# The DRAM round trip of the triangular solve: fewer, wider transfers with an even pitch, in a streaming encoder step

## The chip, the core and the metric

The kernel runs on one core of a Trainium2 chip. The metric is device time in microseconds of one execution. Engines are named as in the profile: PE (TensorE), DVE (VectorE), ACT (ScalarE), POOL (GpSimd) and SP (SyncE, which issues every DMA of this kernel).

## The reference, cut to what matters

One inference step of a one-layer encoder: 2048 prompt tokens and 32 sample tokens of width 1024. After an RMSNorm and the projection `w_in`, the columns go to window attention and to RWKV-7 time mixing; then come `w_out`, cross-attention to 256 memory tokens, and an MLP of width 4096. The change lies in the RWKV part, a recurrence over tokens for each of 8 heads:

```python
def step(S, inp):
    r_t, w_t, k_t, v_t, a_t, b_t = inp
    sa = jnp.einsum('bhij,bhj->bhi', S, a_t)
    S = S * w_t[:, :, None, :] + sa[..., None] * b_t[:, :, None, :] + v_t[..., None] * k_t[:, :, None, :]
    return S, jnp.einsum('bhij,bhj->bhi', S, r_t)
```

The kernel doesn't step token by token. It takes chunks of 64 tokens; within a chunk the term `sa` makes each token depend on the ones before it, which is a unit-triangular system of 64x64 for each head and chunk. Its inverse is what the code below calls the solve.

## The kernel before

**The whole.** A plan written as a string lists the phases in order: Y and Z (projection by `w_in`), R (an RWKV tile of 128 tokens, two chunks; one more, Rs, holds the 32 sample tokens), A (attention), O, C, X, D (output projection and cross-attention), and the MLP behind them. There are 17 RWKV tiles. Each phase runs under a priority, and a scheduler that plans with a timeline of its own lays all instructions out, engine by engine, in a fixed order; each engine then runs its row in that order. So an instruction that waits holds up all that stands behind it on its engine. The dense phases' matmuls (`ps_z`, 24 to a block, three for each of eight weight slices) are the filler between the RWKV tiles' small ones.

**An RWKV tile.** `rwkv_tile` forms `z` and `bk`, multiplies them into `pA`, and ACT copies the triangular part into `ab`: 128 partitions (two heads' 64 rows) by 8 (head pair and chunk) by 64 columns. Then the solve, at highest priority:

- L648 to L650: the 16x16 blocks on the diagonal, 64 of them, go out to the DRAM scratch `lscr`, one block after the other, in eight stores: partitions 16k to 16k+15, all 8 matrices, 16 columns.
- L651 to L653: one gather brings them back as `lt`, one block to a partition, twice (partitions 0 to 63 and 64 to 127).
- L654 to L663: DVE inverts all blocks at once by 15 steps of elimination, each a product into `prd` and an addition into `xt`. The two halves of the partitions hold the even and the odd rows of the inverse.
- L664 to L666: two stores put `xt` into the scratch `xscr`, again block after block.
- L667 to L671: POOL clears `td`, and eight loads put the inverted blocks back on the diagonal, 16 partitions each.
- From L673: a transpose on DVE (`xn`), the matmuls `pgm` and `ptm`, and the same once more widen the 16x16 inverses to 32 and then to 64 rows in `tm`. The serial part over the chunks (`pW`, `pU`, `pS`, `py`) and the normalisation follow.

The scratch tensors `lscr` and `xscr` are made anew for each tile. At the start of the program, POOL clears the eight buffers `rt` (L510). SP's first loads are `par`, then the first token block `xb`, from which PE's first matmuls come.

Of the kernel before, what the change touches and what calls it, by code (L numbers as in the profile page):

```python
# [10 lines left out]
F32 = mybir.dt.float32  # L11
# [6 lines left out]
P = 128  # L18
# [32 lines left out]
def hymba_step_kernel(  # L51
# [9 lines left out]
    V, G, S, T, Q = nc.vector, nc.gpsimd, nc.scalar, nc.tensor, nc.sync  # L61
# [6 lines left out]
    def tt(out, a, b, op, eng=None):  # L68
        (eng or V).tensor_tensor(out, a, b, op=op)  # L69
# [7 lines left out]
    dram = ctx.enter_context(tc.tile_pool(name="dram", bufs=1, space=DRAM))  # L77
# [128 lines left out]
    def setp(k):  # L206
        prs[pcur[0]] = tc.cur_priority
        old, pcur[0] = pcur[0], k
        tc.cur_priority = prs[k]
        return old  # L210
# [39 lines left out]
    rp = rctx.enter_context(tc.tile_pool(name="rp", bufs=1))  # L250
# [204 lines left out]
    def xajob(rp, g, h, t0, tl, src, nb=1, tq=None, tt_=None):  # L455
        sc_f = 128.0 ** -0.5
        if True:
# [47 lines left out]
    rtz = [[[rp.tile([P, 4, 64], F32, name=f"rt{q}{c}{e}", bufs=1) for e in range(2)] for c in range(2)]  # L505
           for q in range(2)]
    for q in range(2):
        for c in range(2):
            for e in range(2):
                G.memset(rtz[q][c][e], 0.0)  # L510
    rcount = [0]

    def halves():
# [2 lines left out]
    def rwkv_tile(g, lo, valid, key, last):  # L516
# [123 lines left out]

        lab(rl_ + "sol")
        pold = setp(PSOL)
        lscr = dram.tile([64, 16, 16], F32, name=f"lscr_{g}_{lo}")
        xscr = dram.tile([64, 16, 16], F32, name=f"xscr_{g}_{lo}")
        if nch == 1:
            V.memset(ab[:, :, 1, :], 0.0)
        ab8 = ab.rearrange("p a c x -> p (a c) x")
        for k in range(8):  # L648
            r0, x0 = 16 * k, 16 * (k % 4)
            Q.dma_start(lscr[8 * k:8 * k + 8].rearrange("q s t -> s q t"), ab8[r0:r0 + 16, :, x0:x0 + 16])  # L650
        lt = rp.tile([P, 16, 16], F32, tag="lt", name="lt", bufs=1)  # L651
        lsr = lscr[:, :, :]
        Q.dma_start(lt, bass.AP(lsr.tensor, lsr.offset, [[0, 2], [256, 64], [1, 256]]))  # L653
        xt = rp.tile([P, 8, 16], F32, tag="xt", name="xt", bufs=1)  # L654
        V.tensor_copy(xt, xt0.rearrange("p (a b) -> p a b", a=8))
        for s in range(15):
# [4 lines left out]
            tt(pv_, xt[:, 0:ni, s:s + 1].broadcast_to([P, ni, m]),  # L661
               lt[:, s, None, s + 1:16].broadcast_to([P, ni, m]), MUL)
            tt(xt[:, 0:ni, s + 1:16], xt[:, 0:ni, s + 1:16], pv_, ADD)  # L663
        xs2 = xscr.rearrange("n (i q) t -> q n i t", q=2)  # L664
        for q in range(2):
            Q.dma_start(xs2[q], xt[64 * q:64 * q + 64])  # L666
        td = rp.tile([P, 8, 32], F32, tag="td", name="td", bufs=1)  # L667
        G.memset(td, 0.0)
        for k in range(8):
            r0, x0 = 16 * k, 16 * (k % 2)  # L670
            Q.dma_start(td[r0:r0 + 16, :, x0:x0 + 16], xscr[8 * k:8 * k + 8].rearrange("q r t -> r q t"))  # L671
        st = 3 - nch
        blk = [(pr, c) for c in range(nch) for pr in range(4)]  # L673
        tm = rp.tile([P, 4, 2, 64], F32, tag="tm", name="tm", bufs=TMB)
# [190 lines left out]
    def rstep(g, i):  # L865
        if g == "s":
            s0 = rp.tile([P, 4, 64], F32, tag="sn", name="sn_s", bufs=SNB)
            Q.dma_start(s0, swkv)
            st8["s"] = (s0, None, None)
            rwkv_tile(0, 0, NS, "s", swo)  # L870
        else:
            if g == 0 and i == 0:
                p0 = rp.tile([P, 4, 64], F32, tag="sn", name="sn_p", bufs=SNB)
                V.memset(p0, 0.0)
                st8["p"] = (p0, None, None)
            lo = i * P + (NS if g == 0 else 0)
            rwkv_tile(g, lo, P, "p", pwkv if (g == 3 and i == 3) else None)
# [43 lines left out]
    for it in PLAN.split():  # L921
        k = it[0]
# [5 lines left out]
        elif k in "RA":  # L928
            g = it[1] if it[1] == "s" else int(it[1])
# [235 lines left out]
```

## Time and profile before

| | |
|---|---|
| three timed runs | 3285.52, 3291.79, 3298.22 us (median 3291.79) |
| profiled execution | 3291.38 us, of which the span from first to last instruction is 3289.6 |
| PE busy | 3046.8 us, 93% of the span |
| DVE, ACT, POOL busy | 58%, 38%, 31% |
| mean granted TensorE clock | 0.958 |

The page gives busy time by engine, 40 equal slices of the span (82.2 us each), the chain of work that ended last, and the costliest groups. The views behind it cut the span into stretches, list waits by who waited for whom, and show instructions one by one. A busy share of PE counts a matmul that runs at half clock as busy too.

### The profile page before, as it was taken

What the parts mean: (1) busy time and instruction counts of PE and PEld (TensorE: products, weight loads), DVE (VectorE), ACT (ScalarE), POOL (GpSimd) and SP (SyncE); (2) the same over time, 40 slices, a digit from 0 to 9 for tenths busy, and PEclk for the clock granted to TensorE, in tenths of its full rate; (3) what the DMA queues carried; (4) which work ended last, traced back from release to release, by engine and by line L of the source; (5) the groups of instructions that cost most, each with busy time, mean ns of one, the idle gap of its engine ahead of it and who ended that gap; (6) DMA issues with size and microseconds to landing.
All of it is one profiled execution on the core that took longest, in us unless ns stands there. A gap on an engine that the chain in (4) does not pass through costs nothing.

```text
span 3289.6 us, 64991 instructions
## 1 busy us (share of the span) xinstructions
PE 3046.8 (93%) x25605; PEld 2851.5 (87%) x25605; DVE 1895.3 (58%) x4482; ACT 1247.3 (38%) x2824; POOL 1018.4 (31%) x1034
## 2 busy tenths in 40 slices
PE   8988888888978998889988999999999999999998
PEld 7877766777767887778978999999999999999998
DVE  4577887876777566774334644444446654444446
ACT  5354555443454454445443312222224322222223
POOL 3543353334344343434444511111112521111111
PEclk9989988999989999989989999999999999999999
DMA  5433333323333453436766211111113211111112
GB/s 174 137 87 96 95 115 106 89 86 109 103 108 109 130 161 105 118 98 205 229 213 197 75 41 46 46 52 40 52 39 105 72 52 46 45 52 52 44 47 90
DMA packets 338660, 317.98 MB, mean 97 GB/s; under 512 B 84490, under 2 KB 260146, under 8 KB 338354
## 3 DMA queue, kind: packets, MB, share of 16 engines
q1 hardware_dynamic: 338354, 313.83, 31.1%
q8 instruction: 201, 3.29, 0.4%
q14 instruction: 105, 0.86, 0.1%
HBM read 245.21 MB, written 68.77 MB: 95 GB/s over the span
## 4 chain that ended last, share of the span: by engine, by line
PE 63%; DVE 15%; DMA 11%; ACT 4%; issue 3%; SPq 2%; POOL 1%; DVEq 0%; ACTq 0%; POOLq 0%
PE ps_up L236 7%; PE ps_dn L995 7%; PE ps_up L235 7%; PE ps_up L234 7%; PE ps_dn L997 7%; PE ps_dn L996 7%; PE ps_z L234 4%; PE ps_z L236 4%; PE ps_z L235 4%; DMA lt<-lscr 3%; DVE z L69 2%; DVE prd L69 1%; DVE xt L69 1%; DMA xscr<-xt 1%; SPq L650 1%
## 5 line engine op out<-in xcount | busy, mean ns | idle before, releaser
L234 PE MATMUL ps_z<-xh,w_h 128*128 128x256 f32 (+1 forms) x2368 | 721.7, 305 | 81.2 <-DVE zo L69 31.8
L235 PE MATMUL ps_z<-xl,w_h 128*128 128x256 f32 (+1 forms) x2368 | 711.3, 300 | 1.8 <-DVE xl L72 1.8
L236 PE MATMUL ps_z<-xh,w_l 128*128 128x256 f32 (+1 forms) x2368 | 708.2, 299 | 0.0
L66 ACT ACTIVATE w_h<-w_raw 128x512 fp32r<-128x512 f32 x576 | 345.3, 626 | 794.5 <-PE ps_up L235 258.5
L69 DVE TENSOR_TENSOR x<-ps_dn,x 128x352 f32<-128x352 f32 (+1 forms) x768 | 389.6, 516 | 365.8 <-PE ps_dn L997 362.1
L234 PEld LDWEIGHTS ps_z<-xh,w_h 128*128 128x128 f32 x2368 | 474.9, 201 | 106.5 <-DVE zo L69 27.7
L69 POOL TENSOR_TENSOR w_l<-w_raw,w_h 128x512 fp32r<-128x512 f32 x300 | 396.3, 1335 | 550.5 <-ACT w_h L66 513.4
L69 POOL TENSOR_TENSOR rl<-rl 128x352 f32<-128x352 f32 (+1 forms) x192 | 161.5, 842 | 1136.9 <-ACT uh L66 1136.9
L236 PE MATMUL ps_up<-fh,w_l 128*128 128x352 f32 (+1 forms) x1536 | 495.6, 323 | 1.3 <-DVE w_l L69 1.2
L995 PE MATMUL ps_dn<-uh,w_h 128*128 128x352 f32 (+1 forms) x1536 | 492.9, 321 | 4.1 <-DVE x L69 3.0
L996 PE MATMUL ps_dn<-ul,w_h 128*128 128x352 f32 (+1 forms) x1536 | 490.8, 320 | 4.9 <-DVE ul L69 4.9
L234 PE MATMUL ps_up<-fh,w_h 128*128 128x352 f32 (+1 forms) x1536 | 493.3, 321 | 0.4 <-DVE zo L69 0.4
L235 PE MATMUL ps_up<-fl,w_h 128*128 128x352 f32 (+1 forms) x1536 | 491.1, 320 | 0.5 <-DVE fl L72 0.5
L997 PE MATMUL ps_dn<-uh,w_l 128*128 128x352 f32 (+1 forms) x1536 | 490.5, 320 | 0.0
L235 PEld LDWEIGHTS ps_z<-xl,w_h 128*128 128x128 f32 x2368 | 474.1, 200 | 18.5 <-issue 11.0
L236 PEld LDWEIGHTS ps_z<-xh,w_l 128*128 128x128 f32 x2368 | 473.9, 200 | 13.4 <-issue 9.4
L69 DVE TENSOR_TENSOR w_l<-w_raw,w_h 128x512 fp32r<-128x512 f32 x276 | 198.4, 738 | 228.1 <-ACT w_h L66 228.0
L996 PEld LDWEIGHTS ps_dn<-ul,w_h 128*128 128x128 f32 x1536 | 289.6, 189 | 5.5 <-DVE ul L69 5.2
L995 PEld LDWEIGHTS ps_dn<-uh,w_h 128*128 128x128 f32 x1536 | 288.7, 188 | 6.1 <-DVE x L69 2.5
L236 PEld LDWEIGHTS ps_up<-fh,w_l 128*128 128x128 f32 x1536 | 288.4, 188 | 2.1 <-DVE w_l L69 1.9
L235 PEld LDWEIGHTS ps_up<-fl,w_h 128*128 128x128 f32 x1536 | 288.5, 188 | 1.1 <-DVE fl L72 0.8
L234 PEld LDWEIGHTS ps_up<-fh,w_h 128*128 128x128 f32 x1536 | 288.2, 188 | 1.2 <-DVE zo L69 0.6
(246 smaller groups left out, 4516.7 us busy)
## 6 DMA issues: line engine op xcount, KB each, us to landing
w_raw<-in_win SPq DMA_DIRECT2D x160, 256.0 KB, 3.0
w_raw<-in_wup SPq DMA_DIRECT2D x136, 256.0 KB, 2.7
w_raw<-in_wdn SPq DMA_DIRECT2D x136, 256.0 KB, 2.9
w_raw<-in_wout SPq DMA_DIRECT2D x64, 256.0 KB, 3.6
zrw<-zo SPq DMA_DIRECT2D x84, 128.0 KB, 3.4
zin<-zrw SPq DMA_DIRECT2D x16, 512.0 KB
w_raw<-in_wcq SPq DMA_DIRECT2D x32, 256.0 KB, 3.4
w_raw<-in_wco SPq DMA_DIRECT2D x32, 256.0 KB, 3.3
```

Source lines behind the costliest of these rows:

```text
L66: S.activation(out, in_, func, **kw)
L69: (eng or V).tensor_tensor(out, a, b, op=op)
L234: T.matmul(ps, lhsT=a, rhs=c, start=(k == 0), stop=False)
L235: T.matmul(ps, lhsT=a, rhs=d, start=False, stop=False)
L236: T.matmul(ps, lhsT=b, rhs=c, start=False, stop=(k == nk - 1))
L650: Q.dma_start(lscr[8 * k:8 * k + 8].rearrange("q s t -> s q t"), ab8[r0:r0 + 16, :, x0:x0 + 16])
L995: T.matmul(ps[:, 0:n], lhsT=wh[:, ms], rhs=us[i][0], start=(i == 0), stop=False)
L996: T.matmul(ps[:, 0:n], lhsT=wh[:, ms], rhs=us[i][1], start=False, stop=False)
L997: T.matmul(ps[:, 0:n], lhsT=wl[:, ms], rhs=us[i][0], start=False, stop=(i == 1))
```

## The change

The scratch takes a form in which whole rows can be moved.

- **Out.** `lscr` holds whole 64x64 matrices, 4160 numbers apart; block n of 16x16 then begins at 1040 n, and its rows are 64 apart. `ab` goes out whole, in two stores of 64 partitions (each 64 x 8 pieces of 64 numbers). Stored before were the diagonal blocks alone.
- **Gather.** Two loads, one for each half of `lt`, take 976 numbers in a row for each of the 64 blocks: its 16 rows of 64, of which the elimination reads the first 16 columns. `lt` is now 1024 wide instead of 256.
- **Inverse back.** `xscr` has a pitch of 32 to a row and 528 to a block, so that two blocks stand on the diagonal of a 32x32 matrix. Two such scratch tensors are made once, filled with zeros by four stores at the start of the program, and used in turn. The two stores of `xt` write the blocks; the zeros beside them stay. Four loads bring 32 partitions of `td` each, zeros included, and the memset of `td` is gone.

```diff
+    xscrs = [dram.tile([64, 528], F32, name=f"xscr{q}") for q in range(2)]
+    for q in range(2):
+        xz = xscrs[q][:, :]
+        zr_ = rtz[0][0][0].rearrange("p a b -> p (a b)")
+        Q.dma_start(bass.AP(xz.tensor, xz.offset, [[256, P], [1, 256]]), zr_)
+        Q.dma_start(bass.AP(xz.tensor, xz.offset + 256 * P, [[256, 4], [1, 256]]), zr_[0:4])
...
-        lscr = dram.tile([64, 16, 16], F32, name=f"lscr_{g}_{lo}")
-        xscr = dram.tile([64, 16, 16], F32, name=f"xscr_{g}_{lo}")
+        lscr = dram.tile([64, 1040], F32, name=f"lscr_{g}_{lo}")
...
-        for k in range(8):
-            r0, x0 = 16 * k, 16 * (k % 4)
-            Q.dma_start(lscr[8 * k:8 * k + 8].rearrange("q s t -> s q t"), ab8[r0:r0 + 16, :, x0:x0 + 16])
-        lt = rp.tile([P, 16, 16], F32, tag="lt", name="lt", bufs=1)
-        lsr = lscr[:, :, :]
-        Q.dma_start(lt, bass.AP(lsr.tensor, lsr.offset, [[0, 2], [256, 64], [1, 256]]))
+        lsr = lscr[:, :]
+        for h in range(2):
+            Q.dma_start(bass.AP(lsr.tensor, lsr.offset + 4160 * h, [[64, 64], [8320, 8], [1, 64]]),
+                        ab8[64 * h:64 * h + 64])
+        lt_ = rp.tile([P, 1024], F32, tag="lt", name="lt", bufs=1)
+        lt = lt_.rearrange("p (a b) -> p a b", a=16)
+        for q in range(2):
+            Q.dma_start(lt_[64 * q:64 * q + 64, 0:976], lscr[:, 0:976])
...
-        xs2 = xscr.rearrange("n (i q) t -> q n i t", q=2)
+        xscr = xscrs[rcount[0] % 2]
+        xsr = xscr[:, :]
         for q in range(2):
-            Q.dma_start(xs2[q], xt[64 * q:64 * q + 64])
+            Q.dma_start(bass.AP(xsr.tensor, xsr.offset + 32 * q, [[528, 64], [64, 8], [1, 16]]),
+                        xt[64 * q:64 * q + 64])
         td = rp.tile([P, 8, 32], F32, tag="td", name="td", bufs=1)
-        G.memset(td, 0.0)
-        for k in range(8):
-            r0, x0 = 16 * k, 16 * (k % 2)
-            Q.dma_start(td[r0:r0 + 16, :, x0:x0 + 16], xscr[8 * k:8 * k + 8].rearrange("q r t -> r q t"))
+        for k in range(4):
+            Q.dma_start(td[32 * k:32 * k + 32], bass.AP(xsr.tensor, xsr.offset + 1056 * k, [[32, 32], [4224, 8], [1, 32]]))
```

The scheduler lays the whole program out anew, so the order moves on every engine. On SP, in tile R11 (128 tokens from column 128 of group 1; `w_raw` are weight loads, `zrw` stores of projections), the order before was:

```order
L650 DMA lscr_128_8735<-ab 16x8x16 x8
L361 DMA zrw_92<-zo 128x256
L653 DMA lt<-lscr_128_8735 128x1x256
L257 DMA w_raw<-in_win 128x512
L361 DMA zrw_92<-zo 128x256
L257 DMA w_raw<-in_win 128x512
L529 DMA zv<-zrw_91 128x4x128
L361 DMA zrw_92<-zo 128x256
L666 DMA xscr_128_8736<-xt 512x1x16 x2
L527 DMA zl<-zrw_91 128x2x128
L671 DMA td<-xscr_128_8736 16x8x16 x8
```

The same place on SP in the changed kernel:

```order
L655 DMA lscr_128_8675<-ab 64x8x64 x2
L660 DMA lt<-lscr_128_8675 64x976 x2
L361 DMA zrw_92<-zo 128x256
L257 DMA w_raw<-in_win 128x512
L535 DMA zv<-zrw_91 128x4x128
L361 DMA zrw_92<-zo 128x256
L257 DMA w_raw<-in_win 128x512
L870 DMA mscr_95<-ao 128x4x128
L800 DMA vf<-zqkv_87 128x128
L674 DMA xscr_144<-xt 64x8x16 x2
L533 DMA zl<-zrw_91 128x2x128
L678 DMA td<-xscr_144 32x8x32 x4
```

The gather stands directly behind the stores, where a `zrw` store stood between; other loads moved to between the gather and the xscr stores.

On DVE in the same tile, from the last product out of `pA` (`z`) to the first elimination step (`prd`), before:

```order
L69 TENSOR_TENSOR z_8641<-pA,cst 64x512
L846 TENSOR_SCALAR sc<-sc,sm 128x256 x2
L72 SCALAR_TENSOR_TENSOR zo<-zo,omu,zm 128x256
L353 COPY zm<-zm 128x1
L353 COPY zm<-carry 128x1
L69 TENSOR_TENSOR sv<-tp,pcl 64x4x64 x2
L69 TENSOR_TENSOR zo<-ps_z,rms_acc 128x256
L72 SCALAR_TENSOR_TENSOR zo<-zo,omu,zm 128x256
L360 COPY carry<-zm 128x1
L69 TENSOR_TENSOR prd<-xt,lt 128x15
```

And in the changed kernel:

```order
L69 TENSOR_TENSOR z_8581<-pA,cst 64x512
L735 COPY ws<-pW 128x256
L69 TENSOR_TENSOR zo<-ps_z,rms_acc 128x256
L72 SCALAR_TENSOR_TENSOR zo<-zo,omu,zm 128x256
L353 COPY zm<-zm 128x1
L353 COPY zm<-carry 128x1
L741 COPY uv<-pU 64x4x64
L69 TENSOR_TENSOR prd<-xt,lt 128x15
```

Fewer rows stand ahead of `prd`, and two of them (`ws`, `uv`) belong to the serial part of the tile before.

On SP at the start of the program, before (`xb` is the first token block):

```order
L93 DMA par<-in_par 128x104
L280 DMA xb<-in_xT 128x2x272 x4
L257 DMA w_raw<-in_win 128x512 x2
L271 DMA xa<-in_xT 128x3x272
```

And in the changed kernel:

```order
L93 DMA par<-in_par 128x104
L515 DMA xscr_143<-rt_127 128x256
L516 DMA xscr_143<-rt_127 4x256
L515 DMA xscr_144<-rt_127 128x256
L516 DMA xscr_144<-rt_127 4x256
L280 DMA xb<-in_xT 128x2x272 x4
```

The four stores of zeros stand ahead of the first token block.

## Rows read from the trace of the kernel before

**Rows 1.** The page: span, busy time by engine, PE and its clock in slices.

```profile
span 3289.6 us, 64991 instructions
PE 3046.8 (93%) x25605; PEld 2851.5 (87%) x25605; DVE 1895.3 (58%) x4482; ACT 1247.3 (38%) x2824; POOL 1018.4 (31%) x1034
PE   8988888888978998889988999999999999999998
PEclk9989988999989999989989999999999999999999
```

**Rows 2.** Stretches: sums of stages A, B, C; then A to C in R00, R01, R03.

```profile
core 0: us, PE busy (x) PEld busy (x) DVE busy (x) ACT busy (x) POOL busy (x), PEclk, DMA share, GB/s
sum 195.44, PE 183.45 PEld 157.88 DVE 86.52 ACT 108.00 POOL 54.31; mean PE 10.79 PEld 9.29 DVE 5.09 ACT 6.35 POOL 3.19
sum 235.22, PE 194.39 PEld 162.57 DVE 222.95 ACT 122.27 POOL 77.78; mean PE 11.43 PEld 9.56 DVE 13.11 ACT 7.19 POOL 4.58
sum 203.49, PE 167.27 PEld 140.12 DVE 146.93 ACT 118.21 POOL 73.54; mean PE 9.84 PEld 8.24 DVE 8.64 ACT 6.95 POOL 4.33
169.14:208.73 39.59, 34.49 (x260) 29.97 (x260) 29.35 (x108) 27.21 (x75) 18.42 (x21) 0.83 0.31 85
244.47:280.75 36.28, 34.85 (x337) 29.03 (x335) 27.78 (x104) 21.11 (x50) 10.45 (x9) 1.00 0.34 88
445.38:492.45 47.07, 34.95 (x299) 28.23 (x296) 37.38 (x98) 32.40 (x79) 24.26 (x26) 0.82 0.46 135
```

**Rows 3.** Waits from 160 to 1520 us: us in total, times, longest.

```profile
DVE prd L69 <- DMA lt<-lscr: 75.6, 17, 7.0
DVE xn L679 <- DMA td<-xscr: 16.8, 7, 5.0
PE pgm L225 <- DVE xn L679: 39.6, 16, 5.3
```

**Rows 4.** Instructions: R11's transfers and what follows; gathers of R00 and R33.

```profile
606.16 3.64 SPq L650 DMA_DIRECT2D lscr<-ab  x8
611.08 0.54 SPq L653 DMA_DIRECT2D lt<-lscr  x1
616.55 0.17 DVE L69 TENSOR_TENSOR prd<-xt,lt 128x15 f32<-128x15 f32 x1 [2.62 <-DMA lt<-lscr]
625.47 1.63 SPq L666 DMA_DIRECT2D xscr<-xt  x2
628.67 3.64 SPq L671 DMA_DIRECT2D td<-xscr  x8
633.75 0.45 DVE L679 STREAM_TRANSPOSE xn<-td 128x256 f32<-128x256 f32 x1 [1.32 <-DMA td<-xscr]
...
174.69 0.61 SPq L653 DMA_DIRECT2D lt<-lscr  x1
182.60 1.08 DVE L69 TENSOR_TENSOR prd<-xt,lt 128x15 f32<-128x15 f32 x1 [0.63 <-DMA lt<-lscr]
1446.60 0.54 SPq L653 DMA_DIRECT2D lt<-lscr  x1
1452.39 0.73 DVE L69 TENSOR_TENSOR prd<-xt,lt 128x15 f32<-128x15 f32 x1 [4.69 <-DMA lt<-lscr]
```

**Rows 5.** DMA issues: KB each, median us to landing; then ns to issue, min/median/max.

```profile
w_raw<-in_win SPq DMA_DIRECT2D x160, 256.0 KB, 3.0
w_raw<-in_wup SPq DMA_DIRECT2D x136, 256.0 KB, 2.7
zrw<-zo SPq DMA_DIRECT2D x84, 128.0 KB, 3.4
lt<-lscr SPq DMA_DIRECT2D x17, 128.0 KB
xscr<-xt SPq DMA_DIRECT2D x34, 32.0 KB, 2.2
L671 SPq DMA_DIRECT2D td<-xscr x136: 303/429/2014, 202.7 to 1479.2; - x136
L666 SPq DMA_DIRECT2D xscr<-xt x34: 527/602/2010, 199.8 to 1472.5; - x34
```

**Rows 6.** Stretch within R13's gather, issued at 749.36 (columns as in rows 2).

```profile
752.00:753.50 1.50, 1.50 (x47) 1.37 (x44) 0.00 (x0) 0.00 (x0) 1.50 (x2) 1.00 0.13 48
```

**Rows 7.** Instructions on PE: two matmuls of the filler that follow each other.

```profile
190.77 0.28 PE L234 MATMUL ps_z<-xh,w_h 128*128 128x256 f32 x1
190.88 0.28 PE L235 MATMUL ps_z<-xl,w_h 128*128 128x256 f32 x1
```

**Rows 8.** Instructions at the start: SP, POOL's clearing of rt, PE's first matmul.

```profile
0.74 0.40 SPq L93 DMA_DIRECT2D par<-in_par  x1
1.20 1.95 SPq L280 DMA_DIRECT2D xb<-in_xT  x4
1.02 2.40 POOL L510 MEMSET rt<- 128x256 f32 x8
9.04 0.59 PE L234 MATMUL ps_z<-xh,w_h 128*128 128x272 f32 x1 [9.04 <-ACT w_h L66]
```

## The prediction

> **What bounds the kernel now.** The page first [rows 1]: PE is busy 93% of the span, and its tenths show two halves. From about 1890 us on (the last 17 slices) nearly every slice is a 9 in PE and in PEclk; nothing that this change touches runs there. Before that, in the stretch where the seventeen RWKV tiles run (169 to 1498 us, slices 3 to 19), PE stands mostly at 8 tenths, and the granted clock falls to 8 in places. Whatever the change is worth is therefore read from that stretch.
>
> Next I cut each tile's solve into three stages by the trace's own marks and summed the 17 of each [rows 2]: A, from the issue of the first lscr store to the first elimination product `prd` on DVE; B, the elimination, to the last `xt`; C, from there to the first `pgm` matmul. A takes 195.4 us in all (11.5 per tile), B 235.2, C 203.5: 634.2 in sum, 37.3 per tile. PE is busy 183.5, 194.4 and 167.3 us of them, so it idles 12.0, 40.8 and 36.2 us: 89 us, or 5.2 per tile. DVE is busy only 86.5 of A's 195.4 us but 223.0 of B's 235.2. So A is a wait on transfers that PE's other matmuls cover almost wholly, B is bound by DVE's own work, and C is mixed.
>
> The waits say what ends them [rows 3]: DVE stands 75.6 us, 17 times, before `prd` for the gather `lt<-lscr`, and 16.8 us, 7 times, before the transpose for `td<-xscr`; PE's largest wait is for that transpose's output, 39.6 us.
>
> **Where a tile's transfer time goes.** In tile R11 [rows 4] the eight lscr stores take SP 3.64 us to issue; the gather is issued 4.92 us after the first of them, and DVE gets its data 5.47 us later. Behind the elimination, two xscr stores are issued at 625.47, the first td load at 628.67, the eight take 3.64 us, and the transpose starts at 633.75.
>
> The gather is odd: it moves 128 KB in about 5.5 us, while a 256 KB weight load lands 3.0 us after its issue [rows 5]. In tile R13 it can be seen almost alone [rows 6]: between 752.0 and 753.5 us the DMA share is 0.13, two of 16 DMA engines, at 48 GB/s. Its access pattern starts with a dimension of size 2, the two copies. (The Trainium skill, "DMA: Bandwidth & Descriptors", Rules for kernel authors, says this: an outermost dimension of size c under 16, such as a leading zero-stride broadcast, confines the transfer to at most c engines. The 0.13 agrees; were the rule wrong, the rival "bytes" below would be the forecast.)
>
> **The change part by part.**
>
> *Stores of ab.* Two issues in place of eight, of 512 pieces each. The nearest row with 512 pieces is the xscr store, 0.60 us to issue and 2.2 us to landing, though with 64-byte pieces (32 KB); for 128 KB in one store it is zrw, landing in 3.4 [rows 5]. First store to gather: 0.6 plus 2.2 to 3.4, so 2.8 to 4.0; I take 3.2, since 128 KB in many pieces stands between the two and nearer the first in shape. Before, it is stage A less the gather, 11.5 - 5.8 = 5.7, the 5.8 being the mean of the 17 gathers, from issue to `prd` (5.2 to 7.9; the first and the last stand in [rows 4]). Saved: 2.5. (The same page of the Trainium skill, Specifications, says that pieces under 512 B fall short of line rate because the engine reads, modifies and writes; the new stores have 256-byte pieces and the td loads 128. The 64-byte xscr stores of the trace land in 2.2 us, which shows no such loss at 32 KB; no run here has 128 KB of such pieces. A doubled landing by that rule would be about 2 us more per tile, 17 x 2 = 34, and would leave little of the gain.)
>
> *Gather.* Two issues, 250 KB each, each with 64 rows outermost. If all 16 engines work, 0.13 of share at 48 GB/s makes about 370 GB/s at full share, so 500 KB take 1.35 us. What remains of the old 5.5 us without its 131 KB at 48 GB/s (2.7 us) is 2.8; with half the data behind the second issue (0.45 us later) that gives 0.45 + 2.8 + 0.7 = 3.9; by the weight load's landing 0.45 + 3.0 = 3.5. I take 3.7, against 5.8. Saved: 2.1. Bounds: 3.1 (a w_raw load at 2.7 plus one issue), and 17 if time went with bytes (rival below).
>
> *Inverse back.* The xscr stores keep their form. Four td loads of 256 pieces replace eight of 128: an issue is 0.43 us at 128 pieces and 0.60 at 512 [rows 4, 5], so about 0.5 each, 2.0 in place of 3.64. Saved: 1.6; with a landing up to 0.5 longer than now, 1.1 at least. The memset of td on POOL, 0.3 us, waits for nothing that matters here and nobody on the path waits for it: nothing.
>
> Per tile 2.5 + 2.1 + 1.6 = 6.2 us of path, 105 us over 17 tiles.
>
> *What the planner made of it.* The path is not the time: PE's and DVE's rows were laid out anew around it. On DVE the planner moved `prd` forward: in R11 a pair of `sc` rows, `zo`, `zm` and `sv` went from ahead of it, `ws` and `uv` came (the order's rows above). On PE I counted the matmuls between a tile's last `pA` and its first `pgm`: 2314 of `ps_z` in the 17 tiles before, 2169 now, and fewer of `pq`, `pss`, `pU` and `pW`. Each kind at its mean time in the trace (`ps_z` of 256 columns about 0.13; at full clock one follows the next after 0.12 [rows 7]), this cover falls from 572 to 529 us, 43 less. That work isn't gone; it stands between the solves and behind them, and costs its time there. So the ceiling is 105 - 43 = 62 us, which fits into the 89 us that PE idles in the stages.
>
> *How much of it arrives.* 40.8 of the 89 us lie in B, where DVE works without a break; an earlier gather shortens the queue that piles up during the 75.6 us wait, but not the 30 elimination steps nor the rows between them. 48 of the 89 lie in A and C, where the transfers themselves end the waits. I take two thirds of the ceiling, 41 us. What the clock gives back where idling shrinks I leave to the range (from A to C the granted clock is 0.83 in R00, where PE idles 5.1 us, and 1.00 in R01, where it idles 1.4 [rows 2]).
>
> *Start.* The four stores of zeros now stand ahead of the first x load on SP and wait for POOL's first memset of `rt`. An issue is about 0.45, so xb goes out at about 2.9 in place of 1.20 [rows 8], and PE's first matmul at 9.04, which hangs on that load, moves by 1.7 us. I book +1.7 in full; it has no cover.
>
> Sum: -41 + 1.7 = -39 us against the profiled execution's 3291.38 (span 3289.6 and 1.8 around it). The median of the three runs is 3291.79, so both bases agree: 3252 us.
>
> **The rivals.**
>
> *Nothing to be had (same).* Stage A is covered by PE's own work already, 183.5 of 195.4 us. If B and the pgm-to-pgm stage set the pace, the queue on DVE only moves: idle that leaves A and C shows up again in the second half of the solve, whose order the planner also redrew. For it: B's DVE at 95%. Against it: DVE's and PE's longest waits are exactly this path. It would give a third of 41 or less: 3280 to 3292.
>
> *All of it (faster).* The whole ceiling and some clock: 62 us, and up to 15 from the clock, less 1.7: 3216. The 15 is what the lowered clock is worth in R00 and R03 alone, 0.17 x 39.6 and 0.18 x 47.1 us [rows 2].
>
> *Bytes (slower).* The gather's time goes with what it moves and not with how many engines it gets: 131 KB at 48 GB/s is then a rate of the reading of fresh scratch, and 500 KB take 10.4 + 2.8 = 13.2 us, or 7.4 more than now. Per tile 7.4 - 2.5 - 1.6 = 3.3 more path and 2.5 less cover, 5.8 x 17 = 99 us: 3392. It decides as soon as the gather lands later than about 7.4 us after its issue (5.8, plus 2.5 and 1.6 saved elsewhere, less 2.5 of cover). Against it: the weight loads' 3.0 us for 256 KB, and the share of 0.13.
>
> *The planner's draw.* Tile by tile PE idles in the three stages between 1.4 us (R01) and 12.1 us (R03) [rows 2], by how the filler happened to fall. 2 to 4 us more per tile from an unlucky order would be 34 to 68 us: 3286 to 3320.
>
> **How the numbers follow.** A measurement of this kernel can tell about 0.5%, 16 us, from no change. Forecast, with 3225 to 3275 as its own range: 0.54. All of it: 0.12. Nothing to be had: 0.18. Planner's draw: 0.12, half of it over 3308. Bytes: 0.04. Faster by over 0.5% is the first two, 0.66; within it, the third, half of the fourth and nothing else, 0.24; slower, 0.10. The range reaches over forecast, most of "all of it" and "nothing": 3212 to 3293.
>
> **What would show it.** DVE's wait before `prd` falls from 75.6 us to about 45; the gather's issue-to-data time is near 3.7 us with a DMA share far over 0.13 while it runs; stage A near 6.9 us and C near 10.4 per tile; PE's idle in A to C falls from 89 to about 45 us; the first matmul starts near 10.7 us; the slices from 1890 us on don't change in length. Wrong is the forecast if A and C are shorter and the last `pgm` is no earlier against the sum of PE's work.

## The result and the profile after

The changed kernel takes 3269.09 us (median of four runs, 3264.26 to 3277.96) against 3289.73 of the kernel before: a ratio of 0.9945 with an interval of 0.9928 to 0.9963. By the medians it is 20.6 us faster, by the interval of the ratio 12 to 24: about half of the 39 that were forecast, or less. Its profiled execution, the fastest of the four, took 3264.26 us, 27.1 less than the profiled one of before; so the sums below account for 27 us, of which some 5 are scatter between executions.

First the page after, beside [rows 1]:

```profile
span 3262.5 us, 64715 instructions
PE 3031.4 (93%) x25605; PEld 2837.5 (87%) x25605; DVE 1894.3 (58%) x4482; ACT 1243.9 (38%) x2824; POOL 1014.4 (31%) x1017
PE   8989888888988998998988999999999999999998
PEclk9999999999988999899989999999999999999999
```

The same PE instructions take 15.4 us less busy time; the row of the granted clock now has four 8s in place of six (mean 0.964, before 0.958). The rest, 11.7 us, is PE idling less: 231.1 us of the span in place of 242.8.

Now the stages of rows 2, the sums of A, B and C over the 17 tiles after:

```profile
sum 150.00, PE 148.38 PEld 127.70 DVE 71.49 ACT 79.34 POOL 42.96; mean PE 8.73 PEld 7.51 DVE 4.21 ACT 4.67 POOL 2.53
sum 245.68, PE 215.55 PEld 183.61 DVE 230.68 ACT 125.49 POOL 68.23; mean PE 12.68 PEld 10.80 DVE 13.57 ACT 7.38 POOL 4.01
sum 149.79, PE 129.03 PEld 112.48 DVE 107.54 ACT 102.05 POOL 47.69; mean PE 7.59 PEld 6.62 DVE 6.33 ACT 6.00 POOL 2.81
```

A is shorter by 45.4 us, C by 53.7, B longer by 10.5: the three together lose 88.7 us. PE idles 52.5 us in them in place of 89.0, so 36.5 of the 88.7 are idle time that went, and 52.2 are matmuls that no longer stand there.

Where they stand now, the other stretches tell. In each pair of lines the first is before, the second after: D (a tile's first `pgm` to the first of its second round), then everything between a tile's last `ptm` and the next tile's first lscr store, then all behind the last tile's solve. A line with three dots stands between views of different stretches.

```profile
sum 275.36, PE 214.09 PEld 190.44 DVE 233.51 ACT 109.99 POOL 152.48; mean PE 12.59 PEld 11.20 DVE 13.74 ACT 6.47 POOL 8.97
...
sum 314.20, PE 300.55 PEld 260.71 DVE 205.01 ACT 149.03 POOL 121.94; mean PE 18.78 PEld 16.29 DVE 12.81 ACT 9.31 POOL 7.62
...
sum 1791.22, PE 1738.39 PEld 1719.16 DVE 845.01 ACT 523.55 POOL 424.29; mean PE 1738.39 PEld 1719.16 DVE 845.01 ACT 523.55 POOL 424.29
```

```profile
sum 246.43, PE 189.96 PEld 161.44 DVE 193.92 ACT 113.79 POOL 132.88; mean PE 11.17 PEld 9.50 DVE 11.41 ACT 6.69 POOL 7.82
...
sum 383.18, PE 349.13 PEld 295.92 DVE 276.93 ACT 169.84 POOL 163.03; mean PE 21.82 PEld 18.49 DVE 17.31 ACT 10.61 POOL 10.19
...
sum 1812.95, PE 1756.25 PEld 1735.88 DVE 851.29 ACT 529.59 POOL 433.17; mean PE 1756.25 PEld 1735.88 DVE 851.29 ACT 529.59 POOL 433.17
```

D gives another 28.9 us. But the stretches between tiles grow by 69.0, 48.6 of it PE's work and 20.4 idle time (sum less busy: 13.7 us before, 34.1 now), and the part behind the last solve grows by 21.7, 17.9 of it work. The remaining stage (second round of widening) loses 2 and the start gains 2: -88.7 - 28.9 - 2 + 69.0 + 21.7 + 2 is -27, the difference of the two spans.

The waits from 160 to 1520 us (us in total, times, longest) answer to [rows 3]; the last two are new in size (15.5 was 7.5, and 8.5 was 3.6):

```profile
DVE prd L69 <- DMA lt<-lscr: 50.4, 17, 4.7
DVE xn L686 <- DMA td<-xscr: 12.8, 11, 2.3
PE pgm L225 <- DVE xn L686: 18.4, 7, 7.7
PE ppt L228 <- DVE sc L853: 15.5, 12, 3.3
PE pU L225 <- DVE ws L735: 8.5, 3, 4.0
```

One tile's transfers in single instructions, R11 after, beside [rows 4] (start, duration, engine, what):

```profile
592.04 1.27 SPq L655 DMA_DIRECT2D lscr<-ab  x2
595.37 1.14 SPq L660 DMA_DIRECT2D lt<-lscr  x2
...
599.71 0.17 DVE L69 TENSOR_TENSOR prd<-xt,lt 128x15 f32<-128x15 f32 x1 [1.60 <-DMA lt<-lscr]
...
610.45 1.30 SPq L674 DMA_DIRECT2D xscr<-xt  x2
...
613.31 1.80 SPq L678 DMA_DIRECT2D td<-xscr  x4
...
616.74 0.45 DVE L686 STREAM_TRANSPOSE xn<-td 128x256 f32<-128x256 f32 x1 [1.37 <-DMA td<-xscr]
```

First store to `prd` is 7.7 us here (before 10.4), first xscr store to the transpose 6.3 (before 8.3). And the start, beside [rows 8]:

```profile
1.19 0.41 SPq L515 DMA_DIRECT2D xscr<-rt  x1
...
2.83 1.93 SPq L280 DMA_DIRECT2D xb<-in_xT  x4
...
11.43 0.60 PE L234 MATMUL ps_z<-xh,w_h 128*128 128x272 f32 x1 [11.43 <-ACT w_h L66]
```

### The profile page after: what moved, and what is told of

It reads as the page before. It is cut to its first block, busy times and chain, and to the rows that moved or that the text cites. A ratio compares the mean times of both kernels' runs of the same rounds, so it can differ in the third digit from the quotient of the medians.

```text
span 3262.5 us, 64715 instructions
## 1 busy us (share of the span) xinstructions
PE 3031.4 (93%) x25605; PEld 2837.5 (87%) x25605; DVE 1894.3 (58%) x4482; ACT 1243.9 (38%) x2824; POOL 1014.4 (31%) x1017
## 4 chain that ended last, share of the span: by engine, by line
PE 62%; DVE 15%; DMA 11%; ACT 6%; issue 3%; POOL 2%; SPq 1%; DVEq 0%; POOLq 0%; ACTq 0%
PE ps_up L236 7%; PE ps_dn L1002 7%; PE ps_up L235 7%; PE ps_dn L1003 7%; PE ps_dn L1004 7%; PE ps_up L234 7%; PE ps_z L234 4%; PE ps_z L236 4%; PE ps_z L235 4%; DVE z L69 2%; DMA lt<-lscr 2%; DVE prd L69 1%; DMA lscr<-ab 1%; DMA xb<-x2scr 1%; ACT xh L66 1%
## 5 line engine op out<-in xcount | busy, mean ns | idle before, releaser
L236 PEld LDWEIGHTS ps_z<-xh,w_l 128*128 128x128 f32 x2368 | 469.6, 198 | 15.5 <-issue 10.8
L1004 PEld LDWEIGHTS ps_dn<-uh,w_l 128*128 128x128 f32 x1536 | 289.2, 188 | 0.2
```

Source lines behind the costliest of these rows:

```text
L236: T.matmul(ps, lhsT=b, rhs=c, start=False, stop=(k == nk - 1))
L1004: T.matmul(ps[:, 0:n], lhsT=wl[:, ms], rhs=us[i][0], start=False, stop=(i == 1))
```

## The experiments

Two theories are held against each other. **The path:** transfer time taken out of a tile's solve is time gained, and the gather's time goes with the number of DMA engines that it gets. **The order:** the transfers matter little, and what moves the time is how the scheduler happens to lay the program out. The scheduler doesn't see how many DMA engines a transfer gets, so a gather can be made quicker or slower with every engine's order as it was; in the traces of each pair below, every engine runs the same operations on the same tiles in the same order. That separates the two. The kernel before was measured again in each set: 3289.9 to 3292.3 us.

### Same order, another gather

In the order of the kernel before, the gather's two copies go inside, under the 64 blocks. Partition p then holds block p//2, so the stores of `xt` take every second partition, and the table `xt0` follows.

```diff
-        Q.dma_start(lt, bass.AP(lsr.tensor, lsr.offset, [[0, 2], [256, 64], [1, 256]]))
+        Q.dma_start(lt, bass.AP(lsr.tensor, lsr.offset, [[256, 64], [0, 2], [1, 256]]))
...
-            Q.dma_start(xs2[q], xt[64 * q:64 * q + 64])
+            Q.dma_start(xs2[q], xt[q::2])
```

> The kernel before with one edit: the gather's two copies alternate from partition to partition, so that its pattern begins with 64 instead of 2. Every engine's row of instructions stays as it was. Theory path (time follows the solve's transfers while the order is fixed): the gather goes from 5.8 to about 3.2 us from issue to prd, 2.6 x 17 = 44 us less path, and 20 to 40 us of it arrive: about 3260. Theory order (the transfers are covered; it was the planner's new order that moved the time): within 8 us of before. If bytes and not the number of engines set the gather, it stays at 5.8 us and so does the time.

Measured: 3243.48 us, ratio 0.9855 (0.9836 to 0.9873): 46 us faster than before, and 26 faster than the whole change. From issue to `prd` the gather takes 3.1 us on the mean of 17, in place of 5.8. The line of the page on busy time, stage A, a stretch inside the gather of R13 (the tile of [rows 6]; issued at 735.84, with no other issue until `prd`; columns as in rows 2), then DVE's wait:

```profile
PE 3025.8 (93%) x25605; PEld 2838.7 (88%) x25605; DVE 1894.1 (58%) x4482; ACT 1246.2 (38%) x2824; POOL 1021.1 (31%) x1034
...
sum 148.43, PE 140.18 PEld 120.03 DVE 86.98 ACT 87.81 POOL 45.05; mean PE 8.25 PEld 7.06 DVE 5.12 ACT 5.17 POOL 2.65
...
736.60:738.00 1.40, 1.40 (x12) 1.18 (x10) 0.00 (x0) 1.06 (x3) 0.29 (x1) 1.00 0.29 94
```

```profile
DVE prd L69 <- DMA lt<-lscr: 28.3, 13, 4.3
```

A is 47.0 us shorter, all other stretches stay within 2.3 us, and the time falls by 46. The DMA share in the gather is 0.29, where it was 0.13 [rows 6]; in other tiles it reads higher (0.50 in R20), but weight loads run beside the gather there. So nearly all of the shorter transfer arrives here, though PE had covered all but 12 us of A. Of the 43 us of matmuls that left A, 26 now stand in B, whose idle time falls from 41 to 17 us (237.53 less 220.44). But idle time is only half of the gain: over the whole span PE idles 26.8 us less, and the same matmuls in the same order take 21.0 us less busy time (3046.8 to 3025.8), at a mean granted clock of 0.962 in place of 0.958. The clock of all five runs lies above that of all nine runs of before in that set (0.961 to 0.963 against 0.956 to 0.960).

The other way: the order of the changed kernel, with each of its two gathers cut so that four blocks are outermost.

```diff
-            Q.dma_start(lt_[64 * q:64 * q + 64, 0:976], lscr[:, 0:976])
+            Q.dma_start(lt_[64 * q:64 * q + 64, 0:976], bass.AP(lsr.tensor, lsr.offset, [[1040, 4], [4160, 16], [1, 976]]))
```

> The changed kernel, each engine's row as it was, but the two wide gathers begin with a dimension of 4 (the blocks come back in another order, so the inverses land in wrong places; all work is done). Four DMA engines in place of 16: 500 KB at 4 x 24 GB/s is 5.2 us in place of 1.3, so 3.9 us more path per tile, 66 in all. Theory path: 35 to 66 us slower than the changed kernel, 3305 to 3335. Theory order: at most 15 us slower, 3285 or less.

Measured: 3346.04 us, ratio 1.0172 (1.0145 to 1.0198), 77 us above the changed kernel. From the first issue to `prd` the two gathers take 9.7 us; A is 230.5 us, 80.5 longer. In R20 of this kernel the share within the gather is 0.25, four engines of 16:

```profile
854.50:858.50 4.00, 4.00 (x47) 3.44 (x46) 0.00 (x0) 1.65 (x4) 1.80 (x2) 1.00 0.25 85
```

A third pair has the wide rows in one gather for both halves, once with the two copies outermost, once inside; the two kernels have one and the same order.

```diff
-        for q in range(2):
-            Q.dma_start(lt_[64 * q:64 * q + 64, 0:976], lscr[:, 0:976])
+        Q.dma_start(lt_[:, 0:976], bass.AP(lsr.tensor, lsr.offset, [[0, 2], [1040, 64], [1, 976]]))
```

> The changed kernel with one wide gather whose pattern begins with the two copies (dimension of 2), and the planner's order redrawn for one DMA less per tile. The gather should take 2.8 + 10.4 = 13 us from issue to prd in place of 4.9. Theory path: 8 us x 17 = 138 us more path, 80 to 140 slower than the changed kernel, 3350 to 3410. Theory order: under 40 slower. It is read against the next run, which has the same order on every engine.

```diff
-        Q.dma_start(lt_[:, 0:976], bass.AP(lsr.tensor, lsr.offset, [[0, 2], [1040, 64], [1, 976]]))
+        Q.dma_start(lt_[:, 0:976], bass.AP(lsr.tensor, lsr.offset, [[1040, 64], [0, 2], [1, 976]]))
...
-                        xt[64 * q:64 * q + 64])
+                        xt[q::2])
```

> As the run with one wide gather, and the same order on every engine, but the two copies alternate from partition to partition, so the pattern begins with 64. One issue in place of two: the gather should take about 4.2 us from issue to prd against 4.9 of the changed kernel. Theory path: 0.7 x 17 = 12 us less path than the changed kernel, up to 12 faster than it, 3255 to 3270, if the redrawn order is as good. Theory order: anything from 3250 to 3290, by the draw.

Measured: 3388.53 us, ratio 1.0294 (1.0271 to 1.0316), with the copies outermost; 3248.19, ratio 0.987 (0.985 to 0.989), with them inside. The difference is 140 us; A takes 283.9 us in the one and 134.5 in the other, 149 apart; the gather 12.9 and 4.1 us. A stretch inside the slow gather of R20, and DVE's wait for all of them:

```profile
884.00:890.00 6.00, 2.71 (x33) 2.42 (x32) 0.00 (x0) 0.41 (x1) 2.51 (x2) 0.92 0.13 52
```

```profile
DVE prd L69 <- DMA lt<-lscr: 178.2, 16, 12.9
```

The share is 0.13 again, at 52 GB/s, where the narrow gather of before had 48. With the copies inside, the gather of the same tile, with nothing issued beside it, had a share of 0.71 at 244 GB/s (801.0 to 803.0 us). The slow gather is the rival "bytes": 13.2 us were worked out for it, and it takes 12.9. It holds with two engines, not with 16; that the total, 3388, is so near the 3392 of the forecast is in part luck, as the order is another than that of the change. (The Trainium skill, "DMA: Bandwidth & Descriptors", Rules for kernel authors, has the number of engines from the slowest dimension; the shares 0.13 and 0.25 for dimensions of 2 and 4 agree.) The order alone explains none of these three pairs. In each, the kernel with less idle time of PE has the higher mean clock: 0.962 against 0.958, 0.964 against 0.945, 0.963 against 0.948.

### One half of the change alone

The way back alone (padded xscr with its zeros at the start, four td loads), the rest as before; the blocks are numbered so that those of one diagonal lie next to each other:

```diff
-            Q.dma_start(lscr[8 * k:8 * k + 8].rearrange("q s t -> s q t"), ab8[r0:r0 + 16, :, x0:x0 + 16])
+            Q.dma_start(lscr[k::8].rearrange("q s t -> s q t"), ab8[r0:r0 + 16, :, x0:x0 + 16])
...
-        G.memset(td, 0.0)
-        for k in range(8):
-            r0, x0 = 16 * k, 16 * (k % 2)
-            Q.dma_start(td[r0:r0 + 16, :, x0:x0 + 16], xscr[8 * k:8 * k + 8].rearrange("q r t -> r q t"))
+        for k in range(4):
+            Q.dma_start(td[32 * k:32 * k + 32], bass.AP(xsr.tensor, xsr.offset + 1056 * k, [[32, 32], [4224, 8], [1, 32]]))
```

> The kernel before with the inverse's way back alone (two scratch tensors with zeros in place, four td loads; the eight lscr stores write the same blocks in another numbering). The order is redrawn: the cover on PE between a tile's last pA and first pgm falls from 572 to 548 us by the counts used in the prediction. Stage C should fall by about 3 us per tile, 50 in all. Theory seen (what the planner sees of a saving it spends by moving filler out of the solve, so little arrives): 3280 to 3300, the zeros' 2.4 us at the start included. Theory all alike (any shorter path arrives, less the cover moved): 50 - 24 - 2.4 = 24 us faster, 3266.

Measured: 3297.55 us, ratio 1.0015 (1.0003 to 1.0028). The time from the end of `xt` to the transpose of `td` shrinks from 10.1 to 7.7 us per tile and stage C from 203.5 to 156.3 us, yet nothing arrives: B is 21 us longer and the stretches between tiles 40. The same kernel, same order, with the copies of its gather inside:

> The kernel before with the inverse's way back and the gather's copies alternating (16 engines); on every engine the same order as the run with the way back alone, so the two differ by the gather alone. Both theories: 40 to 50 us faster than that run, as the gather was at the order of before (46). Against the gather alone at the order of before (3243): theory seen says no faster, 3235 to 3255; theory all alike 24 us faster, 3220.

Measured: 3265.76 us, ratio 0.992 (0.9906 to 0.9934), 32 less than without, but 22 more than the quick gather without the new way back. Both theories had 40 to 50 for this pair, and that was missed: A is 50.5 us shorter (196.0 to 145.6), but B is 11.7 longer and C 5.5. So at a fixed order most of a shorter gather arrives, not always all of it: 46 us of 47, 77 of 80, 140 of 149, and here 32 of 50.

The way out alone (whole `ab`, two wide gathers), the old way back:

```diff
-        for k in range(8):
-            r0, x0 = 16 * k, 16 * (k % 4)
-            Q.dma_start(lscr[8 * k:8 * k + 8].rearrange("q s t -> s q t"), ab8[r0:r0 + 16, :, x0:x0 + 16])
+        for h in range(2):
+            Q.dma_start(bass.AP(lsr.tensor, lsr.offset + 4160 * h, [[64, 64], [8320, 8], [1, 64]]),
+                        ab8[64 * h:64 * h + 64])
...
```

> The kernel before with the way out alone: ab whole in two stores, two wide gathers; the inverse goes back as before, with the blocks numbered anew. No zeros, so no delay at the start. Stage A should fall by about 2 us per tile, 30 to 45 us in all. Theory A (only what shortens stage A is worth time, the way back nothing): as good as the changed kernel with late zeros, 3235 to 3255. Theory both (the way out and the way back are each worth a half): 3262 to 3272.

Measured: 3294.28 us, ratio 1.0005 (0.9991 to 1.0018): nothing again, though A falls by 43.7 us and D by 37. The stretches between tiles and behind the last solve:

```profile
sum 398.89, PE 362.58 PEld 312.11 DVE 260.03 ACT 170.18 POOL 167.75; mean PE 22.66 PEld 19.51 DVE 16.25 ACT 10.64 POOL 10.48
...
sum 1808.72, PE 1756.60 PEld 1737.76 DVE 847.04 ACT 527.48 POOL 432.44; mean PE 1756.60 PEld 1737.76 DVE 847.04 ACT 527.48 POOL 432.44
```

84.7 us longer between tiles, 17.5 behind them. So with the order free, a saving that the scheduler sees is another thing: matmuls move out of the shorter solve (PE does 62 us more work between the tiles and 18 behind them), and with 23 us more idle time between the tiles nothing of the saving is left.

### The zeros at the start

With the four stores of zeros the first matmul starts 2.4 us later (9.04 to 11.43). Put under another priority, they go out behind the first loads:

```diff
+    setp("r")
     for q in range(2):
         xz = xscrs[q][:, :]
...
+    setp("d")
```

> The changed kernel with the four stores of zeros issued behind the first loads. PE's first matmul should be back near 9.0 us from 11.4. The order is redrawn (cover 532 us, as the changed kernel's 529). Without an effect of the draw it is 2.4 us faster than the changed kernel, 3267; anything beyond 8 us from that is the draw.

Measured: 3237.53 us, ratio 0.9832 (0.9815 to 0.9849): 31.6 less than the changed kernel, far over 2.4; the first matmul starts at 9.10. D and what lies behind the last solve:

```profile
sum 222.98, PE 190.26 PEld 160.78 DVE 196.41 ACT 94.37 POOL 126.18; mean PE 11.19 PEld 9.46 DVE 11.55 ACT 5.55 POOL 7.42
...
sum 1795.13, PE 1741.60 PEld 1723.36 DVE 841.16 ACT 521.84 POOL 426.35; mean PE 1741.60 PEld 1723.36 DVE 841.16 ACT 521.84 POOL 426.35
```

Behind the last solve PE does 1741.6 us of work in place of 1756.2 (11372 matmuls, not 11499); the 15 us were done earlier. PE idles 32.7 us of D in place of 56.5, but 17.7 of A in place of 1.6. The transfers of the solve are the same in both kernels and the order is another on every engine, so the order is worth some 30 us here. Is any disturbance of the order worth as much? The zeros alone, unused, in the kernel before, early and late:

> The kernel before with the four stores of zeros at the start alone; nothing reads them. The start should lose 2.4 us as in the changed kernel. The rest does the same work with the same transfers, but the planner redraws the order everywhere (cover 574 us, as before's 572), so this also shows what a mere redraw is worth: 2 us slower than before with no effect of the draw, 3292; anything beyond 8 us from that is the draw.

> A mere redraw of the kernel before: the four stores of zeros, which nothing reads, behind the first loads; no transfer of the solve changes and the start should not be later. If the draw is worth little, 3290 within 5 us. If the two redraws so far are typical (one lost 6 us, one won 29), anything from 3260 to 3310.

Measured: early 3301.05 us, ratio 1.0023 (1.0011 to 1.0036); late 3288.1, ratio 0.9996 (0.9981 to 1.0011). By the traces the early zeros gave every engine another order. The late ones left the order of the kernel before as it was, the four stores and six places among SP's other 1686 transfers apart; so that run was not the redraw that its expectation calls it. Then small memsets on DVE at the start that nobody uses were to disturb the order: one in the kernel before, one and four in the changed kernel with late zeros.

```diff
+    nul0 = const.tile([P, 8], F32, name="nul0")
+    V.memset(nul0, 0.0)
```

> Another redraw of the kernel before: one memset of 8 columns on DVE at the start, about 0.1 us, read by nobody; the planner's order differs behind it on every engine. Expected as for the redraw with late zeros: 3290 within 5 us if the draw is worth little, else 3260 to 3310.

> A redraw of the changed kernel: zeros behind the first loads, and one memset of 8 columns on DVE at the start, read by nobody. If the changed kernel's own order was a poor draw, this lies well under 3267 (3269 less 2.4 at the start), as the run with late zeros did (3238); if that one was the lucky draw, 3260 to 3275.

> A second redraw of the changed kernel: zeros behind the first loads, and four memsets of 8 columns on DVE at the start, read by nobody. As for the redraw with one memset: well under 3267 if the changed kernel's own order was a poor draw, 3260 to 3275 if not. With the two redraws of before and the earlier ones there are then four orders of either kernel; if the rest of the change, beside the gather, is worth something, the means lie more than 46 us apart.

Measured: 3290.16 us, ratio 0.9998 (0.9983 to 1.0012); 3240.95, ratio 0.9846 (0.9827 to 0.9866); 3239.39, ratio 0.9841 (0.9815 to 0.9867). The traces show that none of the three disturbed it: beside the added memsets, every engine runs the operations of the kernel without them in the same order (the few places of PE's 25605 that differ are as many as in the pairs of one order above). So these runs don't test what another order is worth. What they show is that one order, measured again in another kernel, comes back within some 3 us. What an order is worth rests on few of them: two of the kernel before (3290 and 3301) and, of the changed kernel, 3269, 3238 and a third, with two of the four zero stores early:

> The changed kernel with two of the four stores of zeros ahead of the first load and two behind. The start loses about 1 us in place of 2.4. If the 30 us between the changed kernel (3269) and the one with late zeros (3238) come from an order that follows from any delay of the first load as the planner sees it, about 3269; if only the changed kernel's own order was unlucky, near 3240. In between would mean that the loss grows with the delay.

Measured: 3247.36 us, ratio 0.9866 (0.9851 to 0.9881), between the two; the first matmul starts at 9.97 us, and the order is again another. The way back alone with its zeros late:

> The kernel before with the way back alone, the zeros behind the first loads. Stage C should fall by 45 us. Theory A: 3285 to 3295, as the way back with early zeros gave 3298 and the zeros at the start alone 3301. Theory both: 3262 to 3272.

Measured: 3289.15 us, ratio 0.9996 (0.9982 to 1.001). So in these three kernels early zeros cost 8 to 32 us more than late ones (the 8 is barely clear of noise: the two intervals, 1.0003 to 1.0028 and 0.9982 to 1.001, still overlap). That is more than their delay, and each time the order is another too; through which decision of the scheduler is not settled. Nor is it settled why the two halves, each worth nothing with late zeros or without zeros, together give 50 to 55 us with late zeros.

### The best of both

The wide single gather on 16 engines, with late zeros:

> The changed kernel with late zeros and one wide gather whose copies alternate (16 engines, one issue in place of two). Against the same with early zeros (3248): 3245 if only the start's 2.4 us come back, about 3220 if late zeros are worth 30 us here too. Against the changed kernel with late zeros (3238): the gather's 0.7 us less per tile make 12 us, 3226.

Measured: 3230.2 us, ratio 0.9815 (0.98 to 0.983): 60 us faster than before, 39 faster than the change as it came. Its page:

```profile
span 3230.9 us, 64670 instructions
PE 3030.7 (94%) x25605; PEld 2841.6 (88%) x25605; DVE 1893.3 (59%) x4482; ACT 1248.1 (39%) x2824; POOL 1012.7 (31%) x1017
```

PE's busy time is that of the changed kernel; the 31.6 us between the two spans are idle time. One gather in place of two is 20.9 us better with early zeros (3269.09 to 3248.19) and 7.3 with late ones (3237.53 to 3230.2); the order differs in both. Early zeros cost 18 us in this form (3248.19 to 3230.2). (The Trainium skill, "DMA: Bandwidth & Descriptors", Rules for kernel authors, says not to split a transfer over halves of the partitions; the sign agrees, though no pair here has one order.)

## Where the prediction held and where it failed

**Where to look, right.** The late slices stayed what they were, and the transfers' own effect lay in the stretch of the tiles; 122 matmuls moved behind the last solve.

**Stores and gather, 4.6 us per tile: measured 2.7.** A went to 8.8 us per tile, not 6.9. From the first store to the gather it takes 3.9 us (predicted 3.2; 3.3 to 3.6 in ten tiles, 4.2 to 5.4 in seven). The gather takes 4.9 (predicted 3.7): one landing is 3.8 us in the median, and the second is issued 0.6 later:

```profile
lt<-lscr SPq DMA_DIRECT2D x34, 244.0 KB, 3.8
...
lscr<-ab SPq DMA_DIRECT2D x34, 128.0 KB, 2.7
```

The term took 2.8 to 3.0 us for a half, as if each had the engines to itself. Both are under way at once: the single gather of 488 KB on 16 engines lands in 4.0 us, little more than one half. The sum's upper bound of 17 us has no working and doesn't fit the 13.2 of its rival; the slow gather took 12.9. The reason behind the term, the number of engines, is what the four pairs at a fixed order showed. (The Trainium skill, "DMA: Bandwidth & Descriptors", Specifications, puts pieces under 512 B below line rate; it gives no size, and the doubled landing, 34 us, was the prediction's own estimate. The stores of 128 KB in 256-byte pieces land in 2.7 us, inside the 2.2 to 3.4 of the sum; zrw stores of 128 KB in 1024-byte pieces land in 1.9 in the same run. So the small pieces may cost something, but no doubling is seen.)

**The way back, 1.6: measured 2.9** from the end of `xt` to the transpose (10.1 to 7.2 us per tile), 2.6 of it between the first td load and the transpose (6.6 to 4.0). Together 5.6 of the 6.2 us of path went, 95 us of 105. That the path came out so near is luck in part: one term was 1.9 too high, the other 1.3 too low.

**The cover, 43: measured 52** (PE's busy time in A to C, 545.1 to 493.0).

**How much arrives, two thirds of 62: this is the step that failed.** Inside the stages it came nearly as said: idle time there fell by 36.5 us, forecast 44 (from 89 to about 45, measured 52.5). But the sum took the moved cover at its plain cost ("costs its time there"), wherever it went, and looked for idle time in the stages alone. Between the tiles, where most of the cover went, idle time grew by 20.4 us. Of PE's gaps there (34.1 us after, 13.7 before) 8.5 are waits for `ws` before `pU`, 4.8 for `sc` before `ppt` and 3.2 for `kka` before `pbo`; before, these were 2.2, none and 2.0. All three are DVE's own work, a tile's serial part and the next tile's preparation. That these come out late because the filler was laid out anew is read from the trace; it was not tried by itself.

PE's idle time by stretch, after less before: A to C -36.5, D -4.8, the last stage +2.9, between +20.4, behind +3.9, start +2.4, together -11.7. So of the 41 us of idle time that were to go, 11.7 went. The other 15.4 of the 27.1 are PE's busy time at a higher granted clock, which the sum had put at nothing and left to its range; without it the miss would be larger, so that the time came even half way is luck in part. This is the rival "nothing to be had" in part (idle that shows up again elsewhere), only in another place than it named: between the tiles, not in the second half of the solve, which got shorter.

Nor is the split a property of the change. With late zeros, the same transfers and another order, A to C lose only 19.5 us of idle time, D loses 28.5 and the stretches between tiles gain 12.2; the whole span loses 29.6, and PE's busy time 25.1. Which decision of the scheduler puts the idle time where it is stays open.

**The start, +1.7: measured 2.4 directly, and some 30 through the order.** Nothing in the profile of before prices the second number, and the sum had no term for it but the rival "planner's draw", whose price was 34 to 68 us. With the zeros late the same change takes 3237.5 to 3241 us, in three kernels of one order, 11 to 15 below the forecast; with the zeros as they were, 17 above. So the forecast fell between two orders of one change, and to give the draw 0.12 as a rival of its own was the wrong form: a change that the scheduler answers with a new order has the draw in every outcome.

**Signs named ahead.** DVE's wait before `prd` came to 50.4 us (said: about 45), A to 8.8 per tile (6.9), the gather to 4.9 (3.7), C to 8.8 per tile (10.4), the first matmul to 11.43 (10.7). The sign of being wrong, A and C shorter and the last `pgm` no earlier against PE's work, didn't show: up to the end of the last solve the time fell by 48.8 us (1498.38 to 1449.55) and PE's work in it by 33.2, so part of the idle time did go.

## What to carry to other kernels

Put the dimension with many entries (64 here) outermost in an access pattern and a repetition of two inside it: that alone, with no byte more and no instruction moved, was worth 46 us here, more than the whole rewrite. Of a gather made shorter or longer at a fixed order, two thirds to nearly all showed in the time; a saving that the scheduler sees comes with another order, which here could take back all of it. So look at the stretches that it moved work to, try the part at a fixed order before crediting or blaming it, and look in the trace whether an order that was meant to change did change. Keep set-up stores off the queue ahead of the first load: in these kernels, early ones went with a slower order each time.

## What was not expected of the hardware

Bytes are cheap once a gather has more engines: with the 64 blocks outermost, one of 488 KB took 4.1 us from issue to `prd`, one of 128 KB 3.1; with the two copies outermost, they took 12.9 and 5.8.

And a median of landings can mislead. With no instruction moved, the `zrw` stores of 128 KB seem to land in 2.5 us after the gather's copies went inside, in place of the 3.4 of [rows 5]:

```profile
zrw<-zo SPq DMA_DIRECT2D x84, 128.0 KB, 2.5
...
lt<-lscr SPq DMA_DIRECT2D x17, 128.0 KB, 2.4
```

But the trace of the kernel before records the landing of only 6 of these 84 stores, that with the copies inside of 73. Of all `zrw` stores, eight have a landing in both traces, and seven of them differ by less than 1 us either way (medians 3.4 and 3.2). So it isn't shown that a transfer on two engines holds up its neighbours. The [rows 5] medians of before rest on few landings too: 28 of 160 for the weight loads, 2 of 34 for the xscr stores, from which the prediction took its 2.2 to 3.4 and its 3.0.
